# Another order for the steps of the recurrent heads and the attention pairs in a decoder layer's mix

## The chip, the cores and the metric

The kernel runs on one core of a Trainium2 chip. The metric is the device time of one execution in microseconds (us). The kernel before took 2167.82 us, the median of three runs (2166.95 to 2168.07). Its profiled execution took 2166.65 us; the span of the profile, from the first to the last instruction, is 2164.9 us.

## What is computed

One decoder layer on x of 2048 tokens by 1024 columns, in float32. After an RMSNorm, one projection feeds two groups of heads that run side by side: four recurrent heads (HGRN2, key and value width 128) and eight heads of sliding-window attention with a sink, handled as four pairs. Their outputs are joined, projected by `w_out`, added to x, and a gated MLP with a causal convolution follows, then a last RMSNorm.

```python
f = lb + (1.0 - lb) * sigmoid(hf);  k = 1.0 - f;  q = hq * 128 ** -0.5
# S_t = diag(f_t) S_{t-1} + k_t v_t^T,   o_t = S_t^T q_t      (four heads, 64-token chunks)
o_hg = rmsnorm(o, hg_norm_w) * silu(hg)
scores = q_att @ k_att.T / 8;  masked to the 128 tokens back;  m = max(max(scores), sink)
o_att = (exp(scores - m) / (sum(exp(scores - m)) + exp(sink - m))) @ v_att
h = x + concat(o_hg, o_att) @ w_out
h = h + (silu(conv(rmsnorm(h) @ w_gate)) * (rmsnorm(h) @ w_up)) @ w_down
out = rmsnorm(h)
```

## The kernel before, in words

Everything is held transposed, features on the 128 partitions and tokens along the free axis. The tokens are done in two halves of 1024 (`hf` 0 and 1, called half one and half two here). A half has a mix (heads and attention), an output projection (`out_proj`, tiles `pop`), and the MLP (`gate_up`, `down`). Each large product is made of three matmuls on split operands: a float32 tile is split into a rounded part and a remainder (`hi`/`lo`, `XH`/`XL`), and hi·hi, hi·lo and lo·hi are summed. `unit` (line 213) does one such product of 1024 by 128 by 1024: 8 x 3 x 2 = 48 matmuls of 512 columns.

A mix is written as Python generators, which are advanced one step at a time; the loop that advances them is what the change touches.

A recurrent head `hgrn` has five steps for heads 0 to 2: (1) the products `f` and `hq` and the gate f; (2) K and Q, the diagonal, and seven levels m = 1, 2, ... 64 in which decayed scores are built up by doubling blocks; (3) the transposed keys `pkn`, the state products `pu` and the chain of states SS; (4) the product `g` for the output gate; (5) the outputs `po`, their norm `on` and the transposes `pot`. Head 3 does its `g` product between K and the levels, so that its steps are: products, K with gate, levels, states, outputs. The tile `QK` that holds Q and K has one buffer: the next head's K (line 539, on VectorE) must wait until the last `po` matmul of the head before (line 675) has read Q.

In a level, VectorE multiplies Q and K by decays (`QK<-QK,f`, line 615), ScalarE copies them to `G` (line 601), TensorE makes `plev` (line 612), ScalarE copies half of it to `moved` (line 580), a DMA that ScalarE issues shifts that to `odd` (line 582), and VectorE writes both halves into `ST` (lines 586 and 589). `plev`, `pdiag`, `pkn`, `pu`, `po` and `pot` share two PSUM banks, so a level's `plev` waits until the one two before it is read out.

An attention pair `attend` has four steps: (1) the product `q`; (2) for two groups of four blocks the scores `psc`, the mask, the maximum, the exponentials (ScalarE, line 482, after a table load) and the division by `den` (VectorE, lines 485 to 487); (3) and (4) for each group the transposes `ppt`, two masked copies (line 499) and the output `poT`.

`split` (line 225 on VectorE) makes the operands of the output projection from six of the eight finished mix tiles. The last pair and the last head write their split operands themselves. The output projection of the half begins on those six, in the order 0, 4, 1, 5, 2, 6, and needs tiles 7 (the last pair) and 3 (the last head) at its end.

The Python order sets priorities, but the sequence on each engine is settled when the program is built: a scheduler places instructions by its own estimate of when their inputs are there, under the buffer limits of the pools. So the `pop` matmuls stand between the last levels of head 3, and a change in the Python order can move rows on every engine. On the chip every engine then runs its own list strictly in that order and waits on semaphores.

Of the kernel before, what the change touches and what calls it, by code (L numbers as in the profile page):

```python
# [19 lines left out]
KT = D // P  # L20
S = 2048
# [4 lines left out]
HG = 4  # L26
ATT_J = 4
# [16 lines left out]
WARM = 12  # L44
TAIL_WARM = 7
LV = 4


@with_exitstack
def hymba_layer(ctx: ExitStack, tc: tile.TileContext, a: dict, out: bass.AP):  # L50
    nc = tc.nc

    def pool(name, bufs=1, space=None, stack=ctx, **kw):
        if space is not None:
            kw["space"] = space
        return stack.enter_context(tc.tile_pool(name=name, bufs=bufs, **kw))
# [12 lines left out]
    def ps(kind, name):  # L69
        return spaces[kind].tile([P, 512], F32, tag=kind, name=name)  # L70
# [109 lines left out]
    def raw4(src):  # L180
        t = wp.tile([P, D], F32, tag="raw", name="raw", bufs=RAW)
        if src is not None:
            nc.sync.dma_start(t, src)
        return t

    def prep(src, slots=False):

        raw = raw4(src)
        hi, lo = [hp.tile([P, D], F32R, tag="m", name=f"w{t}", bufs=KT) if slots else
                  wp.tile([P, D], F32R, tag=t, name=f"w{t}", bufs=2) for t in ("hi", "lo")]  # L190
        nc.scalar.copy(hi, raw)  # L191
        nc.vector.tensor_tensor(lo, raw, hi.bitcast(F32), op=ALU.subtract)  # L192
        return hi, lo
# [26 lines left out]
    def split(src, w=None, eng=None, dst=None):  # L220

        h, l = dst or new_x()
        if w is None:
            nc.scalar.copy(h, src)
            (eng or nc.vector).tensor_tensor(l, src, h.bitcast(F32), op=ALU.subtract)
        else:
            nc.scalar.activation(h, src, AF.Identity, scale=w)
            nc.vector.scalar_tensor_tensor(l, src, w, h.bitcast(F32), op0=ALU.mult, op1=ALU.subtract)
        return h, l
# [170 lines left out]
    def att_keys(hf, kv, invb, p):  # L400

        KS = p.tile([P, 2, P + HALF], F32R, name="KS")
        V = p.tile([P, 1 + TT, P], F32, name="V")
        if hf:
            nc.vector.tensor_copy(KS[:, :, 0:P], kc)
            nc.vector.tensor_copy(V[:, 0], vc)
        kT, vT = [p.tile([P, HALF], F32, tag="t4", name=n, bufs=2) for n in ("kT", "vT")]  # L410
        for jj, dst in ((ATT_J, kT), (ATT_J + 1, vT)):
            o = kv[jj - ATT_J]
            for b, bs in halves():
                nc.vector.tensor_tensor(dst[:, bs], o[b], invb[:, bs], op=ALU.mult)
                nc.scalar.activation(dst[:, bs], dst[:, bs], AF.Identity, bias=C.battn[:, jj:jj + 1])
        for kv in range(2):
            r, other = rows(kv), rows(1 - kv)
            nc.scalar.copy(KS[r, kv, P:], kT[r])
            nc.vector.tensor_tensor(KS[other, kv, P:], kT[r], KS[r, kv, P:].bitcast(F32), op=ALU.subtract)
        for b in range(NB):  # L420
            pv = ps("at", "pv")
            for i in range(4):
                t0 = (b * 4 + i) * P
                nc.tensor.transpose(pv[:, i * P:(i + 1) * P], vT[:, t0:t0 + P], ident)
            nc.scalar.copy(V[:, 1 + 4 * b:5 + 4 * b].rearrange("p a b -> p (a b)"), pv)
        if hf + 1 < NH:
            nc.vector.tensor_copy(kc, KS[:, :, HALF:HALF + P])
            nc.vector.tensor_copy(vc, V[:, TT])
        return KS, V
# [94 lines left out]
    def hgrn(hf, h, X, invb, vs, WG, mix, p, fu=None):  # L524
# [51 lines left out]
        def place(m, pl):  # L576

            plv = pl.rearrange("p (r b c m) -> p r b c m", r=R, c=2, m=m)
            moved, odd = [p.tile([P, R, 64], F32, tag="lv", name=n, bufs=LV) for n in ("moved", "odd")]
            nc.scalar.copy(moved.rearrange("p r (b m) -> p r b m", m=m), plv[:, :, :, 1])  # L580
# [118 lines left out]
    def project_v(hf, parts, X, rs, p):  # L699

        v = p.tile([P, HG, TT, P], F32, name="v")
        for tt in range(TT):
            o = ps("mm", "pvv")
            t = slice(tt * P, (tt + 1) * P)
            for kt in range(KT):
                hi, lo = parts[kt // 2]
                xh, xl = X[kt]
                c = slice((kt % 2) * 512, (kt % 2 + 1) * 512)
                nc.tensor.matmul(o, xh[:, t], hi[:, c], start=kt == 0, stop=False)
                nc.tensor.matmul(o, xl[:, t], hi[:, c], start=False, stop=False)  # L710
                nc.tensor.matmul(o, xh[:, t], lo[:, c], start=False, stop=kt == KT - 1)
            nc.scalar.activation(v[:, :, tt], o.rearrange("p (h d) -> p h d", h=HG), AF.Identity,
                                 scale=rs[:, tt:tt + 1])
        return [v[:, h] for h in range(HG)]
# [481 lines left out]
    X = []  # L1196
    *nxt, summed = X, *head(X)
    for hf in range(NH):
        X, kv, invb, rs, f0 = nxt
        with ExitStack() as st:  # L1200
            p = pool(f"mix{hf}", stack=st, reuse_waits="tile")
            KS, V = att_keys(hf, kv, invb, p)
            mix = [None] * KT
            vs = []
            M, WG = {}, {}
            for h in range(HG):
                hg = hgrn(hf, h, X, invb, vs, WG, mix, p, f0 if h == 0 else None)
                at = attend(hf, h, X, invb, KS, V, mix, p)
                with tc.issue_after(summed.ins) if hf + h == 0 else ExitStack():
                    next(hg)  # L1210
                if h == HG - 1:
                    next(at)
                    next(hg)
                    for kt in (0, 4, 1, 5, 2, 6):
                        M[kt] = split(mix[kt])
                    next(hg)
                elif h == 0:
                    next(at)
                    wv = [prep(a["w_v"][s], s > 1) for s in range(4)]
                    next(hg)  # L1220
                    vs += project_v(hf, wv, X, rs, p)
                else:
                    next(hg)
                    next(at)
                if h < HG - 1:
                    WG[h] = prep(a["w_g"][h])
                next(at)
                next(hg)
                if h < HG - 1:
                    next(hg)  # L1230
                next(at)
                if h < HG - 1:
                    next(at)
                    next(hg)
                else:
                    next(hg)
                    next(at)
            M[7], M[3] = mix[7], mix[3]
        with ExitStack() as st:
            p = pool(f"ffn{hf}", stack=st, reuse_waits="tile")  # L1240
            kept, ops, hs, first, last = out_proj(hf, M, p)
            acts = gate_up(hf, ops, hs, first, last, p)
            nxt = down(hf, kept, acts, p)
# [61 lines left out]
```

## Time and profile before

| what | number |
|---|---|
| median of three runs | 2167.82 us |
| profiled execution | 2166.65 us |
| its span | 2164.9 us |
| TensorE busy, share of the span | 2142.5 us, 99% |
| VectorE busy | 1658.0 us, 77% |
| ScalarE busy | 1091.6 us, 50% |
| granted TensorE clock, mean | 0.998 |

A busy TensorE is not one at its peak, since a matmul is recorded from its start to its modelled end; the idle time, and the clock in each stretch, are what to look at. In half one the mix runs from about 45 to 370 us and in half two from about 1104 to 1455 us; the rows of a mix are alike up to the order of a few of them, so that the same mark can be timed in both halves.

### The profile page before, as it was taken

The numbers are of one execution on the slowest core, as the hardware profiler recorded it, in microseconds if no ns is written. First come the engines' busy times: TensorE is split into PE (matmuls) and PEld (weight loads), VectorE is DVE, ScalarE is ACT, GpSimd is POOL, SyncE is SP. The second block draws the span as 40 slices with busy tenths as digits, with TensorE's granted clock in tenths as the row PEclk, the third lists the DMA queues.
The fourth block names the chain that finished last, engine by engine and source line by source line (L and its number), as shares of the span: only waits on it lengthen the run. The fifth ranks groups of instructions, "written<-read, shape, count | busy, mean of one in ns | idle before, by whom it ended". The sixth has DMA issues, their size and how long they took to land.

```text
span 2164.9 us, 28224 instructions
## 1 busy us (share of the span) xinstructions
PE 2142.5 (99%) x10752; PEld 1790.8 (83%) x10752; DVE 1658.0 (77%) x2446; ACT 1091.6 (50%) x1858; POOL 6.5 (0%) x28
## 2 busy tenths in 40 slices
PE   9999999999999999999999999999999999999998
PEld 7888888888888888888788888878888888888888
DVE  6557888798887878776864688877978888887766
ACT  6456566564444444435624476645544444454353
POOL 1000000000000000000000000000000000000000
PEclk9999999999999999999999999999999999999999
DMA  4111112413232335954631011214233323259643
GB/s 157 49 40 39 44 44 77 141 51 132 88 123 92 106 103 180 384 204 165 204 127 57 32 39 39 79 46 144 66 106 102 117 83 127 93 197 395 225 141 132
DMA packets 94383, 258.04 MB, mean 119 GB/s; under 512 B 11416, under 2 KB 17576, under 8 KB 94248
## 3 DMA queue, kind: packets, MB, share of 16 engines
q1 hardware_dynamic: 88992, 251.30, 33.9%
q10 hardware_dynamic: 5256, 4.94, 0.8%
q8 instruction: 84, 1.38, 0.3%
q14 instruction: 51, 0.42, 0.1%
HBM read 195.10 MB, written 57.15 MB: 117 GB/s over the span
## 4 chain that ended last, share of the span: by engine, by line
PE 93%; DVE 4%; ACT 1%; DMA 1%; issue 1%; SPq 0%; ACTq 0%; DVEq 0%
PE X L888 7%; PE X L889 7%; PE X L890 7%; PE pop L213 7%; PE hq L213 4%; PE f L213 4%; PE q L213 4%; PE Y L890 4%; PE Y L888 4%; PE Y L889 4%; PE g L213 4%; PE pdx L1099 3%; PE pdx L1101 3%; PE pdx L1100 3%; PE pdy L1101 2%; PE pdy L1100 2%
## 5 line engine op out<-in xcount | busy, mean ns | idle before, releaser
L717 ACT CAST whi<-raw 128x1024 fp32r<-128x1024 f32 x88 | 92.8, 1054 | 109.6 <-PE X L889 68.1
L888 PE MATMUL X<-T,whi 128*128 128x512 f32 x352 | 136.9, 389 | 0.0
L889 PE MATMUL X<-T,whi 128*128 128x512 f32 x352 | 136.9, 389 | 0.0
L890 PE MATMUL X<-T,wlo 128*128 128x512 f32 x352 | 136.9, 389 | 0.0
L983 DVE SCALAR_TENSOR_TENSOR y<-ga,cw,y 128x1024 f32<-128x1024 f32 x88 | 112.5, 1281 | 26.0 <-ACT y L981 26.0
L895 ACT COPY u<-X 128x512 f32<-128x512 f32 x88 | 51.6, 586 | 133.6 <-PE X L890 133.4
L191 ACT CAST whi<-raw 128x1024 fp32r<-128x1024 f32 x57 | 59.6, 1051 | 95.7 <-PE q L213 28.1
L718 DVE TENSOR_TENSOR wlo<-raw,whi 128x1024 fp32r<-128x1024 f32 x88 | 107.4, 1221 | 0.0
L192 DVE TENSOR_TENSOR wlo<-raw,whi 128x1024 fp32r<-128x1024 f32 x57 | 69.4, 1221 | 43.2 <-ACT whi L191 42.8
L718 DVE TENSOR_TENSOR xld<-raw,xhd 128x1024 fp32r<-128x1024 f32 x72 | 80.8, 1134 | 21.9 <-ACT xhd L717 21.4
L717 ACT CAST xhd<-raw 128x1024 fp32r<-128x1024 f32 x72 | 69.7, 979 | 44.8 <-DMA raw<-act0T 17.8
L213 PE MATMUL pop<-XH,whi 128*128 128x512 f32 x256 | 84.5, 394 | 0.9 <-ACT XH L520 0.8
L213 PE MATMUL pop<-XL,whi 128*128 128x512 f32 x256 | 85.3, 391 | 0.0
L213 PE MATMUL pop<-XH,wlo 128*128 128x512 f32 x256 | 84.4, 390 | 0.4 <-DVE wlo L192 0.4
L889 PEld LDWEIGHTS X<-T,whi 128*128 128x128 f32 x352 | 66.1, 188 | 13.7
L888 PEld LDWEIGHTS X<-T,whi 128*128 128x128 f32 x352 | 66.1, 188 | 13.7
L890 PEld LDWEIGHTS X<-T,wlo 128*128 128x128 f32 x352 | 66.1, 188 | 13.7
L1099 PE MATMUL pdx<-xhd,hid 128*128 128x512 f32 x192 | 74.4, 391 | 1.0 <-ACT hid L717 1.0
L1100 PE MATMUL pdx<-xld,hid 128*128 128x512 f32 x192 | 74.7, 389 | 0.0
L1101 PE MATMUL pdx<-xhd,lod 128*128 128x512 f32 x192 | 73.7, 389 | 0.0
L615 DVE TENSOR_TENSOR QK<-QK,f 128x1024 f32<-128x1024 f32 x56 | 68.5, 1223 | 4.8 <-ACT G L601 4.2
L888 PE MATMUL X<-T,Sh 128*128 128x512 f32 x176 | 68.7, 390 | 1.5 <-ACT s L895 1.5
(384 smaller groups left out, 6430.1 us busy)
## 6 DMA issues: line engine op xcount, KB each, us to landing
wr<-in_w_down SPq DMA_DIRECT2D x90, 512.0 KB, 5.8
raw<-in_w_gate SPq DMA_DIRECT2D x44, 512.0 KB, 3.6
raw<-in_w_up SPq DMA_DIRECT2D x44, 512.0 KB, 3.5
raw<-act0T SPq DMA_DIRECT2D x20, 512.0 KB, 8.2
raw<-act1T SPq DMA_DIRECT2D x20, 512.0 KB, 6.7
act0B<-y SPq DMA_DIRECT2D x33, 256.0 KB, 2.3
act1B<-y SPq DMA_DIRECT2D x33, 256.0 KB, 2.3
raw<-in_w_out SPq DMA_DIRECT2D x16, 512.0 KB, 7.4
```

The costliest lines, as they stand in the source:

```text
L192: nc.vector.tensor_tensor(lo, raw, hi.bitcast(F32), op=ALU.subtract)
L213: marks["unit"] = nc.tensor.matmul(o[b], w, x[:, bs], start=f, stop=l)
L615: done = nc.vector.tensor_tensor(own, own, Fv.rearrange("p b w -> p w b").unsqueeze(3).to_broadcast([P, 2, nb, m]), op=ALU.mult)
L717: return (nc.scalar.copy(h, src), (eng or nc.vector).tensor_tensor(l, src, h.bitcast(F32), op=ALU.subtract))
L718: (eng or nc.vector).tensor_tensor(l, src, h.bitcast(F32), op=ALU.subtract))
L888: nc.tensor.matmul(o, wh[:, ws], xh, start=i == 0 and not more, stop=False, skip_group_check=more)
L889: nc.tensor.matmul(o, wh[:, ws], xl, start=False, stop=False, skip_group_check=more)
L890: r = nc.tensor.matmul(o, wl[:, ws], xh, start=False, stop=i == 3, skip_group_check=more)
L983: nc.vector.scalar_tensor_tensor(y, g[:, w:w + HALF], C.cw[:, ft, w:w + 1], y, op0=ALU.mult, op1=ALU.add)
L1099: nc.tensor.matmul(o, wh[:, i, c], ah[:, i, cols], start=f, stop=False, skip_group_check=more)
L1100: nc.tensor.matmul(o, wh[:, i, c], al[:, i, cols], start=False, stop=False, skip_group_check=more)
L1101: nc.tensor.matmul(o, wl[:, i, c], ah[:, i, cols], start=False, stop=l, skip_group_check=more)
```

## The change

The nested loop with its cases is replaced by a table: a string of 43 steps, in which `H1` advances recurrent head 1, `A1` advances attention pair 1, `W`, `V` and `G` load and split weights or make v, and `S` makes the six splits. In the same letters the loop before had: H0 A0 W H0 V G0 A0 H0 H0 A0 A0 H0, then H1 H1 A1 G1 A1 H1 H1 A1 A1 H1, the same for 2, and H3 A3 H3 S H3 A3 H3 A3 H3 A3. What is new:

- head 0's outputs come before the last step of pair 0, and the products of head 1 come before that step too;
- the products of head 2 come before the outputs of head 1;
- the six splits come after the levels of head 3 instead of before them.

Nothing is computed otherwise; the number and the shapes of the instructions stay. All generators are made at the start instead of one pair per turn, which issues nothing.

```diff
+ORDER = """
+H0 A0 W0 H0 V0 G0 A0 H0 H0 A0 H0 H1 A0 H1 A1 G1 A1 H1 H1 A1 A1 H2 H1 H2 A2 G2 A2 H2 H2 A2 A2 H2 H3 A3 H3 H3 S A3 H3 A3 H3 A3
+"""
+SPLIT = (0, 4, 1, 5, 2, 6)
...
-            for h in range(HG):
...
-                with tc.issue_after(summed.ins) if hf + h == 0 else ExitStack():
-                    next(hg)
-                if h == HG - 1:
-                    next(at)
-                    next(hg)
-                    for kt in (0, 4, 1, 5, 2, 6):
-                        M[kt] = split(mix[kt])
-                    next(hg)
...
+            for n, step in enumerate(ORDER.split()):
+                i = int(step[1:] or 0)
+                if step[0] == "H":
+                    with tc.issue_after(summed.ins) if hf + n == 0 else ExitStack():
+                        next(heads[i])
+                elif step[0] == "A":
+                    next(pairs[i])
...
+                else:
+                    for kt in SPLIT:
                         M[kt] = split(mix[kt])
```

In the built program the rows outside the two mixes and the first loads of the output projection of half two keep their order on every engine. The lines of the changed kernel stand four lower than those of the kernel before (line 612 becomes 616). Two places matter below.

First, ScalarE in half two, where the levels of head 3 meet the exponentials of pair 3. `G` and `moved` belong to the levels, `es` and `sc,den` to the softmax. Before:

```order
L601 COPY G<-QK 128x1024
L468 COPY sc<-psc 128x256 x2
L484 ACT_TABLE_LOAD
L484 ACTIVATE es<-es 128x8
L482 ACTIVATE sc,den<-sc,m 128x128 x6
L580 COPY moved<-plev 128x256
L482 ACTIVATE sc,den<-sc,m 128x128 x2
L601 COPY G<-QK 128x1024
L582 DMA odd<-moved 124x256
L580 COPY moved<-plev 128x256
```

And now:

```order
L584 COPY moved<-plev 128x256
L605 COPY G<-QK 128x1024
L586 DMA odd<-moved 124x256
L472 COPY sc<-psc 128x256
L584 COPY moved<-plev 128x256
L586 DMA odd<-moved 120x256
L605 COPY G<-QK 128x1024
L488 ACT_TABLE_LOAD
L488 ACTIVATE es<-es 128x8
L472 COPY sc<-psc 128x256
L486 ACTIVATE sc,den<-sc,m 128x128 x8
L584 COPY moved<-plev 128x256
```

The first `G` of the rows before is that of level 8, and the `G` of levels 16, 32 and 64 follow the first group's exponentials. In the rows now the two `G` are those of levels 16 and 32; only level 64 follows the exponentials. Half one had this second order before and keeps it.

Second, TensorE in half two, where head 2 makes its outputs (`po`) between the matmuls of pair 3's product `q`; `poT` is pair 2's last output. Before:

```order
L674 MATMUL po<-v,ST 128x128
L509 MATMUL poT<-pp,V 64x128 x2
L509 MATMUL poT<-po,V 64x128 x2
...
L675 MATMUL po<-SS,QK 128x128
L213 MATMUL q_11388<-XL,whi 128x512
L213 MATMUL q_11389<-XL,whi 128x512
```

And now:

```order
L678 MATMUL po<-v,ST 128x128
L679 MATMUL po<-SS,QK 128x128
L217 MATMUL q_11389<-XH,wlo 128x512
L217 MATMUL q_11388<-XH,whi 128x512
...
L217 MATMUL q_11388<-XL,whi 128x512
L513 MATMUL poT<-pp,V 64x128 x2
L513 MATMUL poT<-po,V 64x128 x2
```

Before, the last `po` stood behind the sixteen `poT` matmuls, with 28 of the 48 `q` matmuls still to come. Now it stands ahead of them, with 37 `q` matmuls to come. In half one it moves the other way: from 49 matmuls ahead of the end of `q` (one of them of `hq`) to 34; the `poT` stand behind it there in both programs.

More of the change, by code (lines that the diff above doesn't have):

```diff
@@ L1205, in hymba_layer @@
             M, WG = {}, {}
-            for h in range(HG):
-                hg = hgrn(hf, h, X, invb, vs, WG, mix, p, f0 if h == 0 else None)
-                at = attend(hf, h, X, invb, KS, V, mix, p)
-                with tc.issue_after(summed.ins) if hf + h == 0 else ExitStack():
-                    next(hg)
-                if h == HG - 1:
-                    next(at)
-                    next(hg)
-                    for kt in (0, 4, 1, 5, 2, 6):
-                        M[kt] = split(mix[kt])
-                    next(hg)
[L1217 to L1238, printed above, removed]
+            heads = [hgrn(hf, h, X, invb, vs, WG, mix, p, f0 if h == 0 else None) for h in range(HG)]
+            pairs = [attend(hf, j, X, invb, KS, V, mix, p) for j in range(ATT_J)]
+            wv = {}
+            for n, step in enumerate(ORDER.split()):
[5 more added lines that the diff above has]
+                    next(pairs[i])
+                elif step[0] == "W":
+                    wv[i] = [prep(a["w_v"][s], s > 1) for s in range(4)]
+                elif step[0] == "V":
+                    vs += project_v(hf, wv[i], X, rs, p)
+                elif step[0] == "G":
+                    WG[i] = prep(a["w_g"][i])
+                else:
+                    for kt in SPLIT:
+                        M[kt] = split(mix[kt])
+            for kt in range(KT):
+                M.setdefault(kt, mix[kt])
         with ExitStack() as st:
```

## The prediction

> **What bounds the kernel now.** The page comes first: which engine is full, and what the chain that ended last is made of.
>
> ```profile
> span 2164.9 us, 28224 instructions
> PE 2142.5 (99%) x10752; PEld 1790.8 (83%) x10752; DVE 1658.0 (77%) x2446; ACT 1091.6 (50%) x1858; POOL 6.5 (0%) x28
> PE 93%; DVE 4%; ACT 1%; DMA 1%; issue 1%; SPq 0%; ACTq 0%; DVEq 0%
> ```
>
> TensorE carries 93% of the chain. A change of order removes no matmul, so it can only win what TensorE idles (2164.9 - 2142.5 = 22.4 us in the whole span) and what it runs at a lower clock. Next come TensorE's waits: who makes it idle, and where.
>
> ```profile
> PE plev L612 <- ACT G L601: 2.0, 2, 1.3
> PE plev L612 <- DVE ST L586: 1.8, 1, 1.8
> PE ppt L496 <- DVE sc L469: 1.8, 1, 1.8
> PE poT L509 <- DVE y L171: 1.4, 1, 1.4
> PE pop L213 <- ACT XH L520: 0.8, 1, 0.8
> PE poT L509 <- DVE m L475: 0.6, 1, 0.6
> ```
>
> All six are names of a mix, and their sum is 8.4 us. The view of busy time by stretches says where they lie; the columns are busy TensorE, weight loads, VectorE, ScalarE, GpSimd, granted clock, DMA share and GB/s.
>
> ```profile
> 350.00:360.00 10.00, 7.86 (x76) 6.80 (x75) 9.79 (x22) 6.29 (x20) 0.00 (x0) 1.00 0.04 11
> 360.00:370.00 10.00, 8.62 (x82) 7.69 (x82) 7.99 (x24) 4.76 (x26) 0.00 (x0) 1.00 0.01 2
> 1415.00:1425.00 10.00, 7.51 (x63) 6.29 (x62) 7.56 (x17) 7.59 (x25) 0.00 (x0) 0.90 0.12 35
> 1425.00:1435.00 10.00, 7.34 (x73) 6.15 (x67) 6.67 (x16) 6.47 (x24) 0.00 (x0) 0.75 0.01 3
> ```
>
> Both ends of a mix starve TensorE, half two's more (5.15 us idle in 20 against 3.52), and only there the clock falls. In the earlier parts of the mixes no wait of TensorE is listed, so nothing can be won there, only lost. To price the difference I time the same marks in both halves: the second product of head 3 (`hq`), the first `g` matmul after it, and the first `pst` behind the output projection.
>
> ```profile
> 277.72 5.67 PE hq L213 x25
> 1347.66 4.54 PE hq L213 x20
> 312.63 0.62 PE L213 MATMUL g<-XH,whi 128*128 128x512 f32 x2
> 1383.41 0.61 PE L213 MATMUL g<-XH,whi 128*128 128x512 f32 x2
> 451.07 1.68 PE pst L267 x16
> 1527.77 1.68 PE pst L267 x16
> ```
>
> From `g` to `pst` half one takes 451.07 - 312.63 = 138.44 us and half two 1527.77 - 1383.41 = 144.36: 5.92 more for the same work. From `hq` to `g` it is 34.91 against 35.75: 0.84 more. This is the size of what an order can do here.
>
> **Why half two's end is longer.** Two causes, each with rows. The first is when head 3 may start. Its K waits for the last `po` of head 2.
>
> ```profile
> 299.57 0.69 DVE L539 TENSOR_SCALAR QK<-f 128x1024 f32<-128x1024 f32 x1 [0.50 <-PE po L675]
> 309.49 1.29 DVE L685 TENSOR_TENSOR on<-po,y 128x512 f32<-128x512 f32 x2
> 312.61 1.29 DVE L436 SCALAR_TENSOR_TENSOR att<-q,invb 128x512 f32<-128x512 f32 x2 [1.83 <-PE q L213]
> 1377.23 0.70 DVE L539 TENSOR_SCALAR QK<-f 128x1024 f32<-128x1024 f32 x1 [5.32 <-PE po L675]
> 1392.54 1.28 DVE L685 TENSOR_TENSOR on<-po,y 128x512 f32<-128x512 f32 x2
> ```
>
> In half one K starts 13.0 us before `q` is done, VectorE has finished head 2's `on` and is idle 1.83 us when `q` arrives. In half two VectorE stood 5.32 us before K, K starts 6.2 us before `q` is done (the first `g` matmul at 1383.41 marks it), and `on` comes 9.1 us after that, among the splits. The second cause is what stands between the levels.
>
> ```profile
> 343.89 1.06 ACT L601 COPY G<-QK 128x1024 f32<-128x1024 f32 x1
> 344.97 1.28 ACT L484 ACT_TABLE_LOAD   x1
> 1414.63 1.28 ACT L484 ACT_TABLE_LOAD   x1
> 1418.34 0.35 ACT L580 COPY moved<-plev 128x256 f32<-128x256 f32 x1
> 1418.73 0.43 DVE L586 COPY_PREDICATED ST<-lmask,plev 128x256 f32<-128x256 uint32 x1 [2.02 <-ACT moved L580]
> 1419.38 1.04 ACT L601 COPY G<-QK 128x1024 f32<-128x1024 f32 x1
> 1426.73 1.05 ACT L601 COPY G<-QK 128x1024 f32<-128x1024 f32 x1 [3.22 <-DVE QK L615]
> ```
>
> In half one the table load for the exponentials comes after the `G` of level 32. In half two it comes at 1414.63, and `moved` of level 4 and the `G` of level 16 stand behind six and eight exponentials: VectorE stops 2.02 us, and the `G` of level 64 is only there at 1426.73. The levels, each waiting on the one before, are interrupted by 4.8 us of softmax (1414.63 to 1419.38) with three levels still to come instead of one.
>
> What idles TensorE there also costs clock:
>
> ```profile
> 1422.00:1424.00 2.00, 0.61 (x3) 0.61 (x4) 2.00 (x7) 1.51 (x3) 0.00 (x0) 0.77 0.23 61
> 1424.00:1426.00 2.00, 2.00 (x38) 1.61 (x37) 2.00 (x4) 0.00 (x0) 0.00 (x0) 0.50 0.20 57
> 1430.00:1432.00 2.00, 2.00 (x23) 2.00 (x21) 1.09 (x3) 0.87 (x5) 0.00 (x0) 0.50 0.03 8
> 358.35 0.39 PE L509 MATMUL poT<-po,V 128*64 128x128 f32 x4
> 1430.56 0.70 PE L509 MATMUL poT<-po,V 128*64 128x128 f32 x4
> ```
>
> At 0.50 the same four `poT` take 0.70 us instead of 0.39. Full half-clock stretches of some 3 us of busy TensorE cost about half their length, so two of them are at most about 3 us of the 5.92; the rest is the idle time.
>
> [...]
>
> **The change part by part.** No instruction is added or removed; every term is a place in the queue.
>
> *Half two, `g` to `pst`.* The levels now run through 32 before the exponentials, as in half one, and `po` ends 37 `q` matmuls before `q`'s end instead of 28, with the sixteen `poT` behind it. So the stretch should take what half one takes: -5.92. Half two has a little more work in it (its first block has a previous one: two more `poT` and two more `psc` matmuls, under 0.1 us each by the rows above): +0.2. Term: **-5.7 us**. Bounds: if TensorE only gets half one's idle time and the rest stays, -1.6 (5.15 - 3.52); if the waits of half two vanish beyond half one's, -5.7 and another 2.
>
> *Half two, `hq` to `g`.* Its order comes near half one's; half of the 0.84 is taken: **-0.4**, bounds 0 and -0.8.
>
> *Half one, end of the mix.* ScalarE's order was already the good one, so nothing is won by that. K of head 3 now waits for a `po` that ends 34 matmuls and one set of `poT` before `q` does, 49 and a set before. The step and the set:
>
> ```profile
> 374.17 65.56 PE pop L213 x289
> 303.19 1.90 PE poT L509 x32
> 300.78 1.22 DVE L192 TENSOR_TENSOR wlo<-raw,whi 128x1024 fp32r<-128x1024 f32 x1
> 300.18 0.68 DVE L534 SCALAR_TENSOR_TENSOR hg<-hq,invb 128x512 f32<-128x512 f32 x1
> ```
>
> 65.56 / 289 = 0.227 us a matmul, so K starts 34 x 0.227 + 1.9 = 9.6 us before the end of `q` instead of 13.0. From K to the end of `on` took 309.49 + 1.29 - 299.57 = 11.2; of that 0.68 and 1.22 are work that now stands ahead of K, which leaves 9.3. It still fits, by 0.3 us, and the 1.83 us of VectorE's idle time at `q` is what it used up. Behind that VectorE's list holds the same instructions up to the levels. The wait of 1.84 us for level 16's `ST` (line 586) stays, since that row still stands behind `den`, the division and level 64's product. **0**, bounds -1 (VectorE's waits between the levels shrink) and +4.2 (below). In half two the row stands ahead of the division, but the end waits for the second group's softmax anyway: 0.
>
> *The earlier parts.* Products of heads 1 and 2 now run ahead of an attention output or the heads' outputs. Their `po` end some ten matmuls (2.3 us) later against `hq`; K of the next head then has a whole `q` product (48 x 0.227 = 10.9 us) and half of `g` to fill the diagonal. Cover is gone only if VectorE is late by several us, and it idles there: **0**, bounds ±1. SP's queue keeps its order, but for the fifth `w_out` load of half two, which passes the first load of x: **0**, no wait of TensorE on a load is listed there.
>
> Sum: -5.7 - 0.4 = **-6.1 us**. Against the profiled execution that is a span of 2158.8 and a time of 2160.6 (2166.65, which is 1.2 under the median). Against the median: **2161.7 us**. A measurement of this kernel can tell about 0.2% (4.3 us) from no change.
>
> **The rivals.**
>
> *The end of half two stays starved.* The softmax and the levels are one load on VectorE and ScalarE; moved, the stall could come back between level 64 and the second `poT`, and the clock could fall once more. For it: VectorE is 9.79 of 10 us busy in half one at 350. Against it: half one shows the same list without loss of clock. Price: 2167.8 less the idle difference of 1.6 and 0.4 = **2165.8**, same. Chance 0.17.
>
> *Half one pays for its later `po`.* In half two K was 21 matmuls later than in half one and the end 5.92 us longer. If that is proportional, half one pays 15/21 of it, 4.2, and half two, 9 matmuls better, gains only 2.5: 2167.8 + 1.7 = **2169.5**, slower than before. It decides as soon as K to `on` needs more than 9.6 us. Against it: the 9.3 us worked out above. Chance 0.09; a half one that becomes wholly like half two would be +5.9 with nothing won, 2173.7.
>
> *Both ends get better.* The waits in both halves before level 64 (1.84 in half one) go too, as spread-out `pop` matmuls let VectorE catch up: -9, **2158.8**. Chance 0.16.
>
> *The moves are hidden anyway*, because the chip's waits reorder nothing and other rows take their place: 0, **2167.8**. Chance 0.05.
>
> **How the numbers follow.** The forecast has 0.53. Range: from 2157 (both ends better) to 2167 (little of it), with about 0.12 above, mostly the later `po`, and 0.06 below. The forecast's own range is 2159.5 to 2164. Faster by over 0.2%, below 2163.5: 0.53 less a twentieth for a short gain, and 0.16 = 0.68. Slower by over 0.2%, above 2172.2: 0.06, from the upper end of the later `po` and from losses in the earlier parts. The rest, 0.26, is within 0.2%.
>
> **What would show it.** In half two, after: ScalarE's table load of the last pair behind the `G` of level 32; VectorE's wait on the last `po` of head 2 well under 5.32 us; a granted clock of 1.00 in the stretch that now shows 0.75; `g` to `pst` near 138.6 us. In half one: `g` to `pst` within 1 us of 138.44, and K about 9.6 us before `q`'s end. It is wrong if half one's stretch grows by more than 2 us, if half two's stays above 142, or if TensorE's waits list names from heads 0 to 2.

## The result, and the profile after

The changed kernel takes 2163.85 us, median of 17 runs (2161.94 to 2165.61); the kernel before took 2167.82 beside it (2166.64 to 2173.19, 17 runs). The ratio is 0.9979, with a 95% interval of 0.9972 to 0.9986: 4.0 us faster by the medians and 4.5 by the ratio, where 6.1 were forecast. The profiled execution took 2162.83 us, its span is 2161.1.

The page of the changed kernel:

```profile
span 2161.1 us, 28226 instructions
PE 2139.7 (99%) x10752; PEld 1788.8 (83%) x10752; DVE 1659.8 (77%) x2446; ACT 1092.0 (51%) x1858; POOL 6.5 (0%) x28
PE 94%; DVE 3%; ACT 1%; DMA 1%; issue 1%; SPq 0%; ACTq 0%; DVEq 0%
```

TensorE idles 21.4 us (2161.1 - 2139.7) instead of 22.4 and is busy 2.8 us less, though it runs the same matmuls: at first sight most of the gain is clock. The experiments below say otherwise. The four longest of its waits in the mixes:

```profile
PE plev L616 <- DVE ST L590: 2.8, 1, 2.8
PE poT L513 <- DVE y L175: 2.8, 2, 1.4
PE plev L616 <- ACT G L605: 1.2, 1, 1.2
PE ppt L500 <- DVE sc L473: 1.0, 1, 1.0
```

The wait for the level-16 row of `ST`, 1.8 us before, is 2.8 now; the waits for `G` have gone from 2.0 to 1.2, for `sc` from 1.8 to 1.0. The wait of 1.4 us before `poT`, which only half one had, now stands in both halves. The busy time by stretches, columns as before:

```profile
350.00:360.00 10.00, 7.16 (x51) 6.33 (x44) 7.65 (x14) 5.99 (x19) 0.00 (x0) 0.83 0.04 11
360.00:370.00 10.00, 9.01 (x86) 8.06 (x84) 7.59 (x20) 6.14 (x34) 0.00 (x0) 1.00 0.01 2
1415.00:1425.00 10.00, 8.79 (x83) 7.30 (x81) 6.84 (x17) 8.00 (x25) 0.00 (x0) 1.00 0.13 36
1425.00:1435.00 10.00, 8.44 (x86) 7.54 (x85) 8.94 (x24) 6.49 (x25) 0.00 (x0) 1.00 0.01 2
356.00:358.00 2.00, 2.00 (x12) 2.00 (x10) 2.00 (x3) 1.30 (x4) 0.00 (x0) 0.50 0.00 0
```

Half two runs at full clock (0.90 and 0.75 before), and half one, which had full clock, now shows a piece at 0.50. The marks, from the timeline: the first `g` of head 3, the first `pst`, and head 3's K, for half one and then half two.

```profile
314.01 0.62 PE L217 MATMUL g<-XH,whi 128*128 128x512 f32 x2
454.07 1.84 PE L271 MATMUL pst<-ones,invb 128*128 128x1 f32 x16
304.33 0.69 DVE L543 TENSOR_SCALAR QK<-f 128x1024 f32<-128x1024 f32 x1 [0.95 <-PE po L679]
1384.74 0.62 PE L217 MATMUL g<-XH,whi 128*128 128x512 f32 x2
1523.94 1.84 PE L271 MATMUL pst<-ones,invb 128*128 128x1 f32 x16
1374.41 0.69 DVE L543 TENSOR_SCALAR QK<-f 128x1024 f32<-128x1024 f32 x1 [0.50 <-PE po L679]
```

(The timeline puts `pst` 0.16 us earlier than the chain, from which the prediction took it; before, its rows are at 450.91 and 1527.61. From here on all stretches are from the timeline.) Half one takes 454.07 - 314.01 = 140.06 us from `g` to `pst`, 1.78 more than before; half two 139.20, 5.00 less. Half two's `hq` to `g` takes 35.26 instead of 35.91, 0.65 less. The rest of the span is no work of the change: its start was 1.6 us longer (the first product of the keys and values 21.83 us instead of 20.25, with a piece at half clock in it: the granted clock from 10 to 20 us is 0.83, and 1.00 before), the part from half one's `pst` to half two 1.0 shorter.

### The profile page after: what moved, and what is told of

Same layout as the page of the kernel before. It is cut to its first block, busy times and chain, and to the rows that moved or that the text cites. A ratio compares the mean times of both kernels' runs of the same rounds, so it can differ in the third digit from the quotient of the medians.

```text
span 2161.1 us, 28226 instructions
## 1 busy us (share of the span) xinstructions
PE 2139.7 (99%) x10752; PEld 1788.8 (83%) x10752; DVE 1659.8 (77%) x2446; ACT 1092.0 (51%) x1858; POOL 6.5 (0%) x28
## 3 DMA queue, kind: packets, MB, share of 16 engines
q8 instruction: 84, 1.38, 0.3%
## 4 chain that ended last, share of the span: by engine, by line
PE 94%; DVE 3%; ACT 1%; DMA 1%; issue 1%; SPq 0%; ACTq 0%; DVEq 0%
PE X L892 7%; PE X L893 7%; PE X L894 7%; PE pop L217 7%; PE q L217 4%; PE f L217 4%; PE hq L217 4%; PE Y L894 4%; PE Y L893 4%; PE Y L892 4%; PE g L217 4%; PE pdx L1103 3%; PE pdx L1105 3%; PE pdx L1104 3%; PE pdy L1105 2%; PE pdy L1103 2%
```

## The experiments

Each kernel of the experiments was timed 5 to 11 times beside the kernel before, on one chip per group, and profiled once. Two numbers of each trace carry the argument: the stretch from `g` to `pst` in each half, and in half two its two parts, since (`g` to `pst`) = (K to `pst`) - (K to `g`). "Half" counts the pieces between `g` and `pst` in which the granted clock was 0.50; in the ten-microsecond stretches a piece appears as 1.7 us of lost clock (0.83 where it lies in one stretch), so each lasts 3.4 us. Elsewhere, leaving out the first and the last ten microseconds, three of the profiles have a piece at 11 us and six have one near 1090 us.

| kernel | half one `g` to `pst` | half | half two K to `g` | K to `pst` | `g` to `pst` | half | ratio to before |
|---|---|---|---|---|---|---|---|
| before | 138.28 | 0 | 6.18 | 150.38 | 144.20 | 2 | 1 |
| the change | 140.06 | 1 | 10.33 | 149.53 | 139.20 | 0 | 0.9979 |
| the change again | 140.29 | 1 | 10.34 | 149.51 | 139.17 | 0 | 0.9974 |
| old order, then new | 139.49 | 1 | 10.34 | 149.51 | 139.17 | 0 | 0.9965 |
| the same again | 139.91 | 1 | 10.33 | 149.54 | 139.21 | 0 | 0.9979 |
| new order, then old | 138.84 | 0 | 6.18 | 150.36 | 144.18 | 2 | 1.0003 |
| head 1's move alone | 143.87 | 2 | 8.34 | 150.59 | 142.25 | 2 | 1.0000 |
| head 2's move alone | 138.26 | 0 | 6.18 | 150.32 | 144.14 | 1 | 0.9999 |
| before, exponentials later | 139.88 | 1 | 6.17 | 149.27 | 143.10 | 2 | 0.9995 |
| the change, K later | 140.48 | 1 | 6.67 | 149.38 | 142.71 | 2 | 0.9992 |
| the change, division later | 139.29 | 0 | 10.34 | 149.51 | 139.17 | 0 | 0.9974 |
| old order, then new, division later | 139.53 | 1 | 10.34 | 149.53 | 139.19 | 0 | 0.9978 |
| the change, `moved` on VectorE | 138.20 | 0 | 10.34 | 149.52 | 139.18 | 0 | 0.9961 |
| the same in both halves | 138.21 | 0 | 10.33 | 149.12 | 138.79 | 0 | 0.9964 |

**The change once more, and the two orders by halves.** The order of a half was made a choice of that half:

```diff
-ORDER = """ (the new order) """
+ORDERS = [" (the old order) ", " (the new order) "]
...
-            for n, step in enumerate(ORDER.split()):
+            for n, step in enumerate(ORDERS[hf].split()):
```

and the other way round for the third.

> The changed kernel once more, beside the three that follow, on the same chip. What it tells apart: whether half one's extra 1.8 us belongs to the order or to the one execution that was profiled. Theory A (the order makes it): VectorE again reaches the level-16 row of ST only behind the division, TensorE waits about 2.8 us for level 64's product, and the stretch from g to pst in half one takes about 140.2 us again, half two 139.4; time 0.998 of before. Theory B (the granted clock comes and goes by itself): the wait is there again, but the half clock behind it may be missing, half one then takes about 138.5.

> Half one with the old order, half two with the new. Theory A (what an order does in one half stays in that half): half one's stretch from g to pst is that of before, 138.4 us, half two's that of the change, 139.4; 1.8 us less than the change, 2162.0 less or 0.9971 of before. Theory B (the stretches change from run to run, not by the order): no difference to the change beyond 0.5 us, 0.998.

> The reverse: half one with the new order, half two with the old. Theory A: half one 140.2 us, half two 144.4; 1.8 us more than before, ratio 1.0008. Theory B: half one's loss is not the order's, so the ratio is 1.000, and half one between 138.4 and 140.2.

Measured: 0.9974 (0.9964 to 0.9984), 0.9965 (0.9953 to 0.9978), 1.0003 (0.9994 to 1.0012). Half two follows its order to 0.05 us in each of them, as theory A says. Half one does not: under the new order it took 138.84 and 140.29, under the old 138.28 and 139.49. The waits of TensorE are the same in both runs of an order, and what differs is the clock. The rows are those of the new order in half one without the clock loss (the run with the new order first; the change itself, above, had it), and of the old order with it (the run with the old order first):

```profile
350.00:360.00 10.00, 7.05 (x63) 5.97 (x63) 9.08 (x21) 6.07 (x20) 0.00 (x0) 1.00 0.04 11
353.90 1.16 PE L615 MATMUL plev<-G 128*128 128x128 f32 x8 [2.86 <-DVE ST L589]
```

```profile
350.00:360.00 10.00, 7.95 (x77) 7.15 (x77) 7.85 (x15) 6.01 (x19) 0.00 (x0) 0.83 0.04 11
354.64 1.16 PE L615 MATMUL plev<-G 128*128 128x128 f32 x8 [1.84 <-DVE ST L589]
```

So both theories hold a part. Like with like, at full clock the new order costs half one 138.84 - 138.28 = 0.56 us. The piece at half clock comes under either order: in the profiles of the new order with that wait it stands in 3 of 4, of the old order in 3 of 5, and it makes half one 1.2 to 1.6 us longer. The profile of before happened to be one without it, that of the change one with it; so 1.2 of its 1.78 us are a piece that either order can have. How often each order has it, these few profiles do not show. The run with the old order first does not settle whether it beats the change: repeated, it came out at 0.9979 (0.9970 to 0.9989), as the change itself.

> Half one with the old order, half two with the new, once more, to settle whether it beats the change. Half one's stretch is expected at 138.3 us with the clock full and 139.5 to 139.9 with a stretch at half, 0.6 us below the change in each case; ratio 0.9968 to 0.9972, 0.0003 below the change, within what five rounds can tell. If it is again at 0.9965 the old order in half one is worth more than the 0.6 us.

**Which move does it.** Each move of heads was made alone, the splits at their old place.

```diff
-H0 A0 ... H0 A0 H0 H1 A0 H1 A1 ... A1 A1 H2 H1 H2 A2 ...
+H0 A0 ... H0 A0 H0 H1 A0 H1 A1 ... A1 A1 H1 H2 H2 A2 ...
```

```diff
-H0 A0 ... H0 A0 H0 H1 A0 H1 A1 ... A1 A1 H2 H1 H2 A2 ...
+H0 A0 ... H0 A0 A0 H0 H1 H1 A1 ... A1 A1 H2 H1 H2 A2 ...
```

> Only the first of the moves of heads: head 1's projections ahead of the last step of head 0, in both halves; head 2 and the splits at their old places. In the built program half two's end then has all levels ahead of the exponentials, as under the whole change, and half one's end is a third order. Theory A (the order of half two's end is what counts, not which move brings it): half two 139 to 140 us from g to pst; half one 138 to 140; ratio 0.997 to 0.999. Rival (head 2's move is what frees head 3 early): half two stays above 142 and the ratio is at 0.999 to 1.001.

> Only the second of the moves of heads: head 2's projections ahead of the last step of head 1, in both halves; head 1 and the splits at their old places. In the built program the end of both halves stands as before: K of head 3 still behind the late po, the exponentials between the levels in half two. If the gain is half two's end and needs K early (theory A): half two from g to pst stays at 143.5 to 144.5 us with clock lost there, half one 138.3 with the clock full or 139.5 to 139.9 with a stretch at half, ratio 0.9995 to 1.0005; then neither move alone gives the gain and both together do. If head 2's move is what matters by itself: half two 139 to 140, ratio 0.9975.

Neither gives anything: 1.0000 (0.9992 to 1.0009) and 0.9999 (0.9990 to 1.0008). With head 1's move alone, half two has all levels through 32 ahead of the exponentials, and still takes 142.25 us: K starts only 8.34 us ahead of `g`. With head 2's move alone K is where it was before, 6.18. Only both together bring K to 10.33. The move of the splits does nothing by itself: with the splits at their old place and the heads at their new ones, the built program has the same rows on every engine.

Head 2's move alone shows a second thing. Its half two has one piece at half clock where before had two, and takes the same time (144.14 and 144.20). Its stretches and its wait on level 64's `G`, which was 1.27 us:

```profile
1415.00:1425.00 10.00, 7.53 (x53) 6.34 (x52) 7.53 (x21) 8.52 (x27) 0.00 (x0) 1.00 0.09 25
1425.00:1435.00 10.00, 6.85 (x84) 6.05 (x84) 7.03 (x15) 5.55 (x21) 0.00 (x0) 0.83 0.05 13
1428.76 1.16 PE L616 MATMUL plev<-G 128*128 128x128 f32 x8 [2.56 <-ACT G L605]
```

TensorE did the work before that wait at full speed and then waited 1.29 us longer. Of the two pieces of before, the first one, which this run lacks, cost nothing: half two's end ran at the pace of VectorE and ScalarE, from K on, not of TensorE.

**The two causes, one by one.** In the kernel before, the exponentials of half two were put behind level 32's `G`, with K as late as it was:

```diff
+            with tc.issue_after(marks["G", 32].ins) if hf == 1 and j == ATT_J - 1 and g == 0 else ExitStack():
                 for kv in range(2):
                     for i in range(4):
                         nc.scalar.activation(sc[:, kv, i], sc[:, kv, i], AF.Exp, ...)
```

and in the changed kernel K was put behind head 2's second product `on`, with the levels still ahead of the exponentials (in the built program level 64 too, which under the change follows them):

```diff
+        with tc.issue_after(marks["on"].ins) if hf == 1 and h == HG - 1 else ExitStack():
             nc.vector.tensor_scalar(K, f, -1.0, 1.0, op0=ALU.mult, op1=ALU.add)
```

> The kernel before, and in half two alone the exponentials of pair 3's first group issued behind the copy G of level 32; head 3's K still waits 5.3 us for the last po of head 2. It tells my two causes of half two's longer end apart. If the softmax between the levels is the cause: VectorE's 2.0 us stop goes, half two from g to pst falls to 139 to 140.5 us and the clock stays full, ratio 0.998. If the late K is the cause: the levels start as late as before, half two stays at 143 to 145, ratio 0.9995 to 1.0005.

> The changed kernel, and in half two alone head 3's K issued behind head 2's second product on, so that it starts late again while all levels still stand ahead of the exponentials. If the late K is the cause: half two from g to pst goes back to 142 to 145 us, ratio 0.9995 to 1.001. If the softmax between the levels is: it stays within 1 us of 139.2, ratio 0.9975 to 0.998. Third reading (only what breaks TensorE's idle into pieces counts, since the clock falls behind a long one): the stretch follows the granted clock, 139 to 140 with it full, 142 and more with 3 us at half.

Measured 0.9995 (0.9986 to 1.0004) and 0.9992 (0.9983 to 1.0001). K and `pst` of half two in the first, and in the second:

```profile
1377.78 0.69 DVE L540 TENSOR_SCALAR QK<-f 128x1024 f32<-128x1024 f32 x1 [5.32 <-PE po L676]
1527.05 1.84 PE L267 MATMUL pst<-ones,invb 128*128 128x1 f32 x16
```

```profile
1379.32 0.68 DVE L544 TENSOR_SCALAR QK<-f 128x1024 f32<-128x1024 f32 x1
1528.70 1.84 PE L271 MATMUL pst<-ones,invb 128*128 128x1 f32 x16
```

From K to `pst` they take 149.27 and 149.38 us, as the change does (149.5), against 150.3 to 150.4 where the exponentials stand between the levels. So the softmax between the levels is worth about 1 us (head 1's move alone has the levels ahead too, in yet another order with a wait of 1.9 us at `psc`, and takes 150.59), and where K starts is worth its own lateness, microsecond for microsecond: in all fourteen profiles K to `pst` in half two lies between 149.1 and 150.6, while K to `g` goes from 6.2 to 10.3. Half two's 5.00 us are 10.33 - 6.18 = 4.15 from the earlier K and 150.38 - 149.53 = 0.85 from the levels (1.11 when the exponentials alone were moved). The third reading, that the stretch follows the clock, goes with the lengths of these two runs (both lost clock and are long) but not with head 2's move alone, and from K to `pst` these two are no longer with two pieces at half clock than the change is with none.

**What level 64 waits for in half one.** VectorE's rows around the division in the changed kernel, and ScalarE's `moved`:

```profile
351.66 0.17 DVE L489 TENSOR_TENSOR den<-den,es 128x8 f32<-128x8 f32 x1 [2.03 <-ACT sc L486]
352.10 1.22 DVE L491 TENSOR_TENSOR sc<-sc,den 128x1024 f32<-128x1024 f32 x1
353.24 1.22 DVE L619 TENSOR_TENSOR QK<-QK,f 128x1024 f32<-128x1024 f32 x1
354.38 0.41 DVE L590 COPY_PREDICATED ST<-lmask,plev 128x256 f32<-128x256 uint32 x1
352.47 0.36 ACT L584 COPY moved<-plev 128x256 f32<-128x256 f32 x1
```

The level-16 row comes last. There are two accumulators for the levels, taken in turn, so the one it reads is the one that level 64's product takes. VectorE idles 2.03 us before `den`, so the row seemed free to go there. The first attempt asked for the division behind the row, in half one:

```diff
+            with tc.issue_after(marks["row", 16].ins) if j == ATT_J - 1 and g == 0 and hf == 0 else ExitStack():
                 nc.vector.tensor_tensor(sc, sc, den.unsqueeze(3).to_broadcast([P, 2, 4, P]), op=ALU.mult)
```

> The changed kernel, with one edge of order more in half one: the division of pair 3's first group is issued behind the level-16 row of ST, so that the row runs in the 2.0 us in which VectorE waits for the exponentials (as it stands in half two already, behind den). TensorE's order is word for word that of the changed kernel. Theory A (level 64's product waits for its accumulator, which the row of level 16 frees): the wait of 2.84 us falls to the 0.7 to 1.2 us until ScalarE's G of level 64, ppt starts some 2 us earlier, and the clock has no window in which to fall: half one from g to pst 137 to 138.5 us in place of 138.8 (clock full) to 140.3 (with a stretch at half), ratio to before 0.9955 to 0.9970. Rival (the next thing is late anyway: pu waits for Kn, whose copy stands behind ScalarE's copies of level 32): the wait moves to pkn and pu, half one 138.8 or more, ratio as the change, 0.9975 to 0.998.

> The same edge under the old order in half one, half two with the new order. There the wait is 1.84 us and VectorE reaches the row late in the same way. Theory A: wait down to 0.7 to 1.2, half one 137 to 138 us, clock at full speed in each execution; ratio 0.995 to 0.9965, the fastest so far. Rival: the wait moves on, no difference to the run without the edge (0.9965).

Both expectations of theory A failed: 0.9974 (0.9964 to 0.9984) and 0.9978 (0.9970 to 0.9987); in the first half one took 139.29 us at full clock, where the change takes 138.84. In the first:

```profile
350.78 0.36 ACT L585 COPY moved<-plev 128x256 f32<-128x256 f32 x1
350.91 1.23 DVE L620 TENSOR_TENSOR QK<-QK,f 128x1024 f32<-128x1024 f32 x1 [0.53 <-ACT G L606]
352.06 0.42 DVE L591 COPY_PREDICATED ST<-lmask,plev 128x256 f32<-128x256 uint32 x1
352.39 1.22 DVE L492 TENSOR_TENSOR sc<-sc,den 128x1024 f32<-128x1024 f32 x1
352.53 1.16 PE L617 MATMUL plev<-G 128*128 128x128 f32 x8 [2.20 <-DVE ST L591]
```

The row did not move into the idle time; the division moved behind it. `moved` and the row read the same accumulator, and the row had waited for `moved` before (2.02 us on line 586 in the prediction's rows); `moved` stands behind eight exponentials on ScalarE. The edit had held back the wrong thing. The second attempt made that one copy on VectorE:

```diff
-            nc.scalar.copy(moved.rearrange("p r (b m) -> p r b m", m=m), plv[:, :, :, 1])
+            copy = nc.vector.tensor_copy if hf == 0 and h == HG - 1 and m == 16 else nc.scalar.copy
+            copy(moved.rearrange("p r (b m) -> p r b m", m=m), plv[:, :, :, 1])
```

> The changed kernel; in half one the copy moved of head 3's level 16 is made by VectorE in place of ScalarE, so that it and the level-16 row of ST run in the 2.0 us in which VectorE waits for the exponentials (the run with the division held back showed the row to wait for moved, behind eight exponentials). Theory A (the accumulator of level 16, freed late, is what level 64's product waits for): the 2.8 us wait falls to about 0.7 (until ScalarE's G of level 64); pkn now stands ahead of ppt and waits some 2 us for VectorE's product of level 64; the net gain is about 1 us, half one 137.8 us with the clock full and 139.2 with a stretch at half (138.8 and 140.1 to 140.5 under the change); ratio 0.9970 to 0.9975. Rival (idle time only moves to pkn, and the stretch at half speed comes as before): 139 to 140.5, 0.9975 to 0.998.

> The same in both halves. In half two the wait for level 64's product is 1.2 us and ends with G, not with the row, and ppt follows 1.0 us later; there pkn ahead of ppt turns these two waits into one of 0.7 and one of some 2 us. Theory A (only the sum of the idle time counts): half two 139 us, within 0.5 of 139.2. Theory C (a long single idle stretch costs clock, two short ones do not): half two now shows, in this execution or in part of the timed ones, a stretch at half clock, 140 to 141 us; ratio 0.001 above the run before it.

Measured 2159.67 us (2158.81 to 2160.90), 0.9961 (0.9947 to 0.9975), lower than either expectation; with the same copy moved in both halves 2160.21, 0.9964 (0.9951 to 0.9976). In the first:

```profile
347.97 0.42 DVE L585 COPY moved<-plev 128x256 f32<-128x256 f32 x1
348.30 0.42 DVE L591 COPY_PREDICATED ST<-lmask,plev 128x256 f32<-128x256 uint32 x1
351.19 1.16 PE L617 MATMUL plev<-G 128*128 128x128 f32 x8 [0.63 <-ACT G L606]
353.51 1.06 PE L654 MATMUL pkn<-ident,QK 128*128 128x128 f32 x8 [1.17 <-DVE QK L620]
350.00:360.00 10.00, 7.51 (x74) 6.58 (x73) 9.49 (x21) 5.88 (x20) 0.00 (x0) 1.00 0.01 3
```

The row is done 1.5 us ahead of `den`, where under the change it was done 3.1 us behind it; the wait of 2.8 us has become one of 0.63 and one of 1.17, and half one takes 138.20 us, 0.64 less than the change at full clock. In neither kernel's profile does a piece at half clock stand in the end of a mix, and the slowest of the five timed runs of the first, 2160.90, is under the fastest of the 25 of the change (2161.54). The ratios lie 0.0013 to 0.0018 apart, 2.8 to 3.9 us; 0.64 is shown by the profiles, and a piece that came in neither of them would be another 1.2 to 1.6. The mean granted clock of every timed run points the same way (0.999 to 1.000 in the five, 0.997 to 0.999 in the 25; one piece is 1.7 of 2160 us, 0.0008), but where the other runs lost clock isn't recorded, and the rest of the difference stays open. In half two the copy gives 0.4 us (138.79) and the time shows no difference. The version with the one copy moved has the lowest median here, though its interval overlaps those of the change.

## Why the prediction was right, and where it was not

*Half two, `g` to `pst`: -5.7, measured -5.00.* The two causes named were the right ones and the experiments separate them, 4.15 us for the late K and 0.85 for the levels. Mis-sized was the step "the stretch should take what half one takes": half one is carried by TensorE there, with K 13.1 us ahead of `g`, while half two stays bound by the work from K on, with K 10.33 ahead. As long as the work from K on takes 149.5 us, 149.5 - 10.33 gives 139.2; only the copy on VectorE in both halves, with 149.12, brought it lower, to 138.79.

*The clock.* "Two of them are at most about 3 of the 5.92; the rest is the idle time" was a bound, and the runs show that at least one piece was worth nothing: with one instead of two the half took the same time (144.14 and 144.20 us), since TensorE then waited 1.29 us longer for what it would have waited for anyway. The gain was not lost clock won back. That both pieces were free isn't shown directly, since no profile with K as late as before had none. All three pieces at the ends of the mixes in the profiles of before and of the change stand behind stretches in which TensorE was partly idle, 2.19 and 1.86 us before and 2.24 in the change, of 3.4 us each (rows in the last section).

*Half two, `hq` to `g`: -0.4, measured -0.65*, inside its bounds.

*Half one: 0, measured +1.78, of which 0.56 at equal clock.* K came 9.68 us before `g` (9.6 forecast), `on` just fitted (VectorE idle 0.15 us at `q`, 1.83 before). Two steps failed. "Behind that VectorE's list holds the same instructions up to the levels. The wait of 1.84 us ... stays" did not hold: the wait is 2.84 us. And the working asked only whether `on` fits before `q`, not whether the levels, which also begin at K, then end later against TensorE's work; at full clock they do, by 0.56. The other 1.2 us are the piece at half clock that comes in some executions of either order, which a single profile could not tell: that the profile of before had none in half one was chance, and the sign named for half one, within 1 us of 138.44, was not met.

*Half two's row ahead of the division: 0.* With the row ahead, level 64 waits 1.21 us there, for `G`; in half one, with the row behind, 2.84. What the row's place is worth was tried in half one only: 0.64 us at full clock, and neither of the two profiles with the copy moved has the piece at half clock there.

*Earlier parts: 0.* The waits list names none of heads 0 to 2.

*The rivals.* "Half one pays for its later `po`" is the mechanism that half one shows, at 0.56 us instead of 4.2. "Both ends get better" did not come with the change; the version with `moved` on VectorE reaches it by another edit, at 2159.7 us (2158.8 was its price). That the moves are hidden is out by the interval of the ratio, 0.9972 to 0.9986. That the end of half two stays starved is out: K's wait on the last `po` fell from 5.32 to 0.50 us, the table load stands behind level 32's `G`, the clock is 1.00.

*The sum.* -6.1 was forecast. At equal clock the two ends give -5.00 + 0.56, and half two's `hq` to `g` -0.65: -5.1, or 0.9976. The two measurements of the change, 0.9979 and 0.9974, lie on both sides of it. One sum of the chances is off: 0.53 less a twentieth and 0.16 make 0.64 to 0.66, not 0.68.

## What to carry to other kernels

Where a stage ends on a chain over several engines, find its first instruction and measure from it: in half two the time from K to the end was the same within 1.5 us in fourteen executions, and everything that moved K moved the end. In half one, where TensorE carried the stage, K came 3.4 us later and the end only 0.56. Before a difference between two profiles is put down to a change, look at the granted clock in both, and compare executions with the same pieces at half speed: 1.2 of half one's 1.8 us were such a piece. And an order edge that is to bring a row forward must sit on what that row waits for: here not on the division behind it, but on a copy on another engine that reads the same accumulator.

## What the runs showed of the hardware that was not expected

The clock fell to half in some executions and not in others with the same order in that half and the same waits to within 0.05 us: behind a wait of 2.84 to 2.86 us in 3 of 4 profiles, behind one of 1.84 in 3 of 5. Behind waits of at most 1.21 us it never did, in half two of the eight profiles with the new order and in half one of the two with `moved` on VectorE; nor behind the 1.38 us before `poT` in the profiles of before and of the change. Each piece was 3.4 us long. After 2.20 us it was absent once (the change, division later), after 1.27 us with 0.58 beside it present once (half two of before). So the length of the last wait alone does not sort these profiles.

Where the pieces begin was read in the same traces. In the profile of before the two of half two begin at 1423.09 and 1429.91 us, 6.82 apart, two lengths of 3.41. In that of the change the two begin at 11.27 and 356.02 us, 344.75 apart, 101 lengths of 3.413. Half one under the new order in two executions, in stretches of that length counted from the pieces of each (columns as before): the run with the new order first, where no piece came in this half, and the change again, where one did.

```profile
348.93:352.34 3.41, 2.11 (x27) 1.50 (x21) 1.56 (x4) 3.41 (x14) 0.00 (x0) 1.00 0.00 0
352.34:355.76 3.42, 1.85 (x16) 1.86 (x17) 3.42 (x7) 0.90 (x4) 0.00 (x0) 1.00 0.11 34
```

```profile
350.42:353.84 3.42, 0.77 (x7) 0.78 (x7) 3.42 (x6) 1.16 (x4) 0.00 (x0) 1.00 0.11 34
353.84:357.25 3.41, 3.41 (x19) 3.41 (x18) 3.19 (x6) 1.65 (x5) 0.00 (x0) 0.50 0.00 0
```

In the first the idle time is split over two stretches, 1.30 and 1.57 us; in the second 2.65 us fall into one, and the next runs at half. The profiles of before and of the change, cut in the same way, show at the ends of their mixes the stretches ahead of the three pieces, each with the stretch that follows it, and, last in each block, the one from 40 to 2130 us with the most idle time that has no piece behind it:

```profile
1419.67:1423.09 3.42, 1.23 (x9) 0.97 (x8) 3.35 (x7) 2.51 (x6) 0.00 (x0) 1.00 0.26 73
1423.09:1426.50 3.41, 3.11 (x40) 2.37 (x40) 3.41 (x7) 0.42 (x1) 0.00 (x0) 0.50 0.11 34
1426.50:1429.91 3.41, 1.55 (x15) 1.34 (x16) 3.41 (x10) 2.58 (x6) 0.00 (x0) 1.00 0.00 0
1429.91:1433.33 3.42, 3.42 (x32) 3.09 (x29) 1.18 (x3) 2.24 (x12) 0.00 (x0) 0.50 0.02 5
351.30:354.71 3.41, 1.77 (x16) 1.77 (x16) 3.41 (x7) 1.40 (x5) 0.00 (x0) 1.00 0.11 34
```

```profile
352.60:356.01 3.41, 1.17 (x10) 1.17 (x11) 3.41 (x7) 0.93 (x4) 0.00 (x0) 1.00 0.12 34
356.01:359.43 3.42, 3.42 (x17) 3.20 (x16) 3.37 (x6) 1.98 (x6) 0.00 (x0) 0.50 0.00 0
1438.04:1441.45 3.41, 2.03 (x26) 1.59 (x26) 3.17 (x13) 0.00 (x0) 0.00 (x0) 1.00 0.02 5
```

Ahead of a piece TensorE idled 2.19, 1.86 and 2.24 us, elsewhere at most 1.64 before and 1.38 in the change. These are few stretches of one kernel: they show neither what sets the clock nor how much likelier the longer wait of the new order makes a piece. What brings the six pieces near 1090 us was not shown either.
